# Rotary step on folded rows, squares summed on another engine, softmax rows in pairs: a hybrid encoder layer on one Trainium2 core

## The chip, the core and the metric

The kernel runs on one core of a Trainium2 chip. A core has TensorE (PE in the profile, with PEld for its weight loads), VectorE (DVE), ScalarE (ACT), GpSimd (POOL) and SyncE (SP), which here only issues transfers; ScalarE issues some transfers too. Each of these runs its instructions in the order in which they were built, and they wait for each other through semaphores. The metric is the device time of one execution in microseconds (us); less is better.

## The reference

One encoder layer in float32 on 1024 tokens of width 1024. One projection feeds two token mixers: group A is windowed attention (8 query heads, 2 key heads, a sink logit per head, rotary on the first 16 of 64 dimensions), group B is neighbourhood attention on a 16 x 64 grid of tokens. After that come an output projection, a gated MLP with a short convolution, and a last norm.

```python
def partial_rope(t, cos, sin):
    half = ROT_DIM // 2          # 8
    x1, x2 = t[..., :half], t[..., half:ROT_DIM]
    return concatenate([x1 * cos - x2 * sin, x2 * cos + x1 * sin, t[..., ROT_DIM:]], -1)

hn = rmsnorm(x, norm_mix)
proj = einsum('bsd,de->bse', hn, w_in)
qa, ka, va, qb, kb, vb = split(proj)
qa, ka = partial_rope(qa, cos, sin), partial_rope(ka, cos, sin)
# group A, per head: scores in a window of |i - j| <= 128, with the sink in the softmax
m = maximum(max(s, -1), sink)
p = exp(s - m)
o = einsum(p, v) / (sum(p, -1) + exp(sink - m))
# group B: p = softmax(scores + relative bias), o = einsum(p, v)
h = x + einsum(concat(rmsnorm(o_a), rmsnorm(o_b)), w_out)
h = h + conv_gated_mlp(rmsnorm(h, norm_ffn), ...)
out = rmsnorm(h, norm_final)
```

## The kernel before

Activations are kept transposed: 128 features on the partitions, 1024 tokens along the row, so a tile is 128x1024. To keep float32 precision each matmul operand is split into a rounded high part (ScalarE) and the rest (VectorE), and each product is three matmuls (`block`, lines 113 to 115).

**Head (up to 50 us).** The input's eight slices `xt` arrive; ScalarE makes the high part `xgh`, VectorE the low part `xgl` (`split_scaled`, line 126). The first two projection tiles use each slice as it comes; the third tile starts when all slices are there. Beside that ScalarE squares each slice and `squares(xts, nc.gpsimd)` sums the squares with seven additions on GpSimd (line 141). TensorE adds the sum over the partitions, and the resulting `rstd1` scales every projection as it leaves PSUM (`evacuate`, line 170).

**Projections.** `Project(m)` makes tile m. Of the first six, 0 and 3 hold one key head (partitions 0 to 63) and one value head, the others two query heads each. The columns are arranged so that in each head every eighth partition, from 0 and from 4, holds a rotated dimension: partition 8r holds x1 and 8r + 4 its partner x2. `post` finishes a tile: `split_v` transposes values, `rotate` does the rotary step, then `split_k` or `split_pair` make the parts and copies that the score matmuls need. `split_pair` leaves a query tile as two operand tiles, of which the first is complete only after its last copy, on SP (line 195); `split_k` issues `kb<-ka` (line 215) and `ka<-kb` (line 217) on SP as well.

**Rotation.** `rotate(t, n)` has two transfers on ScalarE's queue (line 182) put each row's partner into a zeroed tile `u`, then multiplies the whole tile by cosines (ones in the other rows, VectorE, line 183), `u` by signed sines (GpSimd, line 184), and adds them (VectorE, line 185). Two such tiles `u` take turns.

**Attention.** A unit is a block of queries. Score rows run in `softmax`: VectorE adds the mask and takes the minimum `nm` of the negated scores (line 284), ScalarE takes exponentials with their sum `sm` (line 288), VectorE the reciprocal (line 289), GpSimd scales the row (line 290); for group A GpSimd first copies the negated sink into the row's end (line 283). Two rows lie in one tile `p`. Later TensorE transposes the rows (`pt`), which are split again (`ph`, `pl`, lines 295 and 296) and multiplied with the values (`o`, lines 327 and 328). TensorE's order is written out by hand: projections are the filler between attention steps, by `FILL0`, `FILL1` and `RATES`. The order on the other engines and on the queues is made by a scheduler when the kernel is built, from priorities and from when it takes each input to be ready.

Tiles `rc`, `rs`, `u`, the third tile's weights, some tiles `p` and the attention outputs share eight buffers named `mix`.

Of the kernel before, what the change touches and what calls it, by code (L numbers as in the profile page):

```python
# [51 lines left out]
def hybrid_layer(tc, xT, w_in, w_out, w_gate, w_up, w_down, small, sink, rpb, consts, rope, out):  # L52
    nc = tc.nc
    with ExitStack() as ctx:
# [9 lines left out]
        spool = inner("stats", 6)  # L64
# [3 lines left out]
        def big(name, tag, dt=F32):  # L68
            return lpool.tile([128, S], dt, name=name, tag=tag, bufs=slots[tag])
# [65 lines left out]
        def squares(tiles, engine):  # L135
            acc = None
            for t in tiles:
                s2 = tmp("sq")
                nc.scalar.activation(s2, t, AF.Square)
                if acc is not None:  # L140
                    engine.tensor_tensor(s2, s2, acc, op=ALU.add)
                acc = s2
            return acc
# [29 lines left out]
                o = t[:, :].rearrange("p (b r c) -> p r b c", r=ROWS, c=8)[:, 8 * h:8 * h + 8]  # L173
                nc.vector.tensor_tensor(o, v(ps[:, :]), v(rstd1[:, tsl(h)]), op=ALU.mult)

        turned = []

        def rotate(t, n):
            u = turned[0]
            turned.append(turned.pop(0))  # L180
            for i in (0, 4):
                nc.scalar.dma_start(u[i:n:8], t[4 - i:n:8])
            nc.vector.tensor_tensor(t[0:n], t[0:n], rc[0:n], op=ALU.mult)
            nc.gpsimd.tensor_tensor(u[0:n], u[0:n], rs[0:n], op=ALU.mult)
            nc.vector.tensor_tensor(t[0:n], t[0:n], u[0:n], op=ALU.add)

        def split_pair(t):

# [46 lines left out]
        mix = [None] * 8  # L235
# [38 lines left out]
                return lpool.tile([128, 2, 386], F32, name="p", tag="mix", bufs=slots["mix"], padded_shape=[128, 2, 512])  # L274
            return apool.tile([128, 2, 386], F32, name="p", tag="p", bufs=5)

        def softmax(p, j, ps, n, bias, nsink=None):

            w = lambda ap: ap.rearrange("p (c w) -> p c w", w=128)
            with tc.high_priority(offset=50):  # L280
                nm, sm = spool.tile([128, 1], F32, name="nm"), spool.tile([128, 1], F32, name="sm")
                if nsink is not None:
                    nc.gpsimd.tensor_copy(p[:, j, n:n + 1], nsink)
                nc.vector.tensor_tensor_reduce(  # L284
                    out=w(p[:, j, 0:n]), in0=w(ps[:, 0:n]), in1=bias, scale=1.0, scalar=3e38 if nsink is None else nsink,
                    op0=ALU.add, op1=ALU.min, accum_out=nm)
                e = n if nsink is None else n + 1
                nc.scalar.activation(p[:, j, 0:e], p[:, j, 0:e], AF.Exp, bias=nm, scale=-1.0, accum_out=sm)  # L288
                nc.vector.reciprocal(sm, sm)  # L289
                nc.gpsimd.tensor_scalar(p[:, j, 0:n], p[:, j, 0:n], sm, 1.0, op0=ALU.mult, op1=ALU.mult)  # L290

        def split_pt(ps, n):
            ph = apool.tile([128, HALF], F32R, name="ph", tag="ph")
# [5 lines left out]
        def unit_window(g, b):  # L299

            cs, n = near(b), 128 * len(near(b))
            ps4 = [None] * 4
            mask = cst[:, K_MA:K_MA + 384].rearrange("p (c w) -> p c w", w=128)
            mask = mask[:, cs[0] - b + 1:cs[-1] - b + 2]
            st = {}

            def q_step(j):
                def go():
                    if j % 2 == 0:
                        st["p"] = pair_tile(True)  # L310
                    ps, _ = scores(qa[g, j // 2][j % 2], ka[g], b)
                    softmax(st["p"], j % 2, ps, n, mask, nsink[:, 4 * g + j:4 * g + j + 1])
                    ps4[j] = st["p"][:, j % 2, :]
                return go

            def t_step(i):
                def go():
                    if i == 0:
                        st["o"] = bank("o", "o")
                    pt = bank("pt", "pt")  # L320
                    for j in range(4):
                        nc.tensor.transpose(pt[:, j * 128:(j + 1) * 128], ps4[j][:, i * 128:(i + 1) * 128], ident)
                    ph, pl = split_pt(pt, HALF)

                    def v_step():
                        o, v = st["o"], va[g]
                        nc.tensor.matmul(o, v[:, cs[i], :], ph, start=i == 0, stop=False)
                        nc.tensor.matmul(o, v[:, cs[i], :], pl, start=False, stop=i == len(cs) - 1)
                        if i == len(cs) - 1:
                            leave()  # L330
                    return v_step
                return go

            def leave():
                ot = apool.tile([128, 2, 128], F32, name="ot", tag="ot", bufs=1, padded_shape=[128, 4, 128])
                o4 = st["o"][:, :].rearrange("p (j w) -> p j w", w=128)
                for e in range(2):
                    me, other = slice(64 * e, 64 * e + 64), slice(64 - 64 * e, 128 - 64 * e)
                    nc.scalar.activation(ot[me], o4[other, e::2, :], AF.Copy)
                    for i in range(2):  # L340
                        if mix[2 * g + i] is None:
                            mix[2 * g + i] = big("mixa", "mix")
                        nc.vector.tensor_tensor(mix[2 * g + i][me, b * 128:(b + 1) * 128], o4[me, e + 2 * i, :], ot[me, i, :], op=ALU.add)

            return [q_step(j) for j in range(4)], [t_step(i) for i in range(len(cs))]
# [19 lines left out]
        def units_grid(h):  # L365

            ps4 = [None] * NB
            st = {"begun": [False, False]}
            e = 64 * (h % 2)
            me, other = slice(e, e + 64), slice(64 - e, 128 - e)  # L370

            def q_step(b):
                def go():
                    if b == 0:
                        bias_of[h] = bias_of.pop(h, None) or bias_tiles(h)
                    if b == 4 and h < 7:
                        bias_of[h + 1] = bias_tiles(h + 1)
                    x = bias_of[h]
                    if b % 2 == 0:
                        st["p"] = pair_tile()  # L380
                    sel = slice(2, 5, 2) if b == 0 else slice(0, 3, 2) if b == NB - 1 else slice(1, 4)
                    ps, n = scores(qb[h], kb[h], b)
                    softmax(st["p"], b % 2, ps, n, x[:, sel, :])
                    ps4[b] = st["p"][:, b % 2, :]
                return go

# [111 lines left out]
        xts, sqs = [], []  # L498
# [41 lines left out]
        nc.sync.dma_start(par[:, C_SINK:C_END], sink.partition_broadcast(128))  # L540
        nsink = cpool.tile([128, 8], F32, name="nsink")
        nc.vector.tensor_scalar(nsink, par[:, C_SINK:C_END], -1.0, None, op0=ALU.mult)
        rc, rs = big("rc", "mix"), big("rs", "mix")
        nc.sync.dma_start(rc, rope[0])
        nc.sync.dma_start(rs, rope[1])

        for _ in range(2):
            u = big("u", "mix")
            nc.gpsimd.memset(u, 0.0)
            turned.append(u)  # L550

        banks = [[bank("pj", "pj") for _ in range(2)], [bank("o", "o") for _ in range(2)]]
        acc = None
        for k in range(KT):
            if k:
                xg[k] = split_scaled(xts[k], col(C_NMIX + k), "xg", "xg")
            for h in range(2):
                for p, ps in zip(first, banks):
                    block(ps[h], p.w[k], xg[k], h, k == 0, k == KT - 1)
        acc = squares(xts, nc.gpsimd)  # L560
        jobs = [Project(m) for m in range(2, 18)] + [OutA(d) for d in range(KT)]
        third = jobs[0]
        raw, hi, lo = big("raw3", "mix"), big("whi3", "mix", F32R), big("wlo3", "mix", F32R)
# [84 lines left out]
        for g in range(2):  # L648
            for b in range(NB):
                q, t = unit_window(g, b)  # L650
# [49 lines left out]
        for u in range(len(flat)):  # L700
            q, t, need, kind = flat[u]
# [412 lines left out]
        for i, f in enumerate(FO[HEAD:]):  # L1114
            u = Gated(f)
# [99 lines left out]
        for i, (p, j, c) in enumerate(order):  # L1215
            prepare(i + 6, i + 4)
            f, n = PARTS[c]
# [4 lines left out]
            ps = banks[p, j]  # L1222
# [48 lines left out]
def _constants():  # L1271
    import numpy as np

    f = np.float32
    consts = np.zeros((128, K_END), f)
    consts[:, K_ID:K_ID + 128] = np.eye(128, dtype=f)
    q, k = np.arange(128)[:, None], np.arange(128)[None, :]
    ma = np.zeros((128, 3, 128), bool)
    ma[:, 0], ma[:, 1], ma[:, 2] = k >= q, True, k <= q
    consts[:, K_MA:K_MA + 384] = np.where(ma, 0, MASKED).reshape(128, 384)  # L1280
    rq, cq, rk, ck = q // 8, q % 8, k // 8, k % 8
    r0 = np.clip(rq - KH // 2, 0, ROWS - KH)
# [7 lines left out]
    rope = np.zeros((2, 128, S), f)  # L1290
    rope[0] = 1.0
    for e in (0, 64):
        rope[0, e:e + 64:8], rope[0, e + 4:e + 64:8] = cos, cos
        rope[1, e:e + 64:8], rope[1, e + 4:e + 64:8] = -sin, sin
    return consts, rope


# [45 lines left out]
```

## Time and profile before

| What | Value |
|---|---|
| median of 3 runs | 1141.33 us (1141.04 to 1143.16) |
| profiled execution | 1136.96 us, span 1135.0 us |
| granted TensorE clock, mean | 0.986 |
| busy: TensorE, VectorE, ScalarE, GpSimd | 1088.1, 874.7, 550.2, 149.1 us |
| up to 130 us: seven additions of squares on GpSimd (line 141) | 19.6 us |
| up to 130 us: six products with sines on GpSimd (line 184) | 16.9 us |
| up to 130 us: VectorE's two operations of six rotations (lines 183, 185) | 9.7 and 9.7 us |

Rows of the timeline read: start in us, duration in us, engine, line, operation, output and inputs, shapes, count, and in brackets the engine's idle time just before and who ended it. SPq and ACTq are the transfers that SyncE and ScalarE issue. In rows of groups the number behind the bar is busy time in us, then the mean duration of one in ns, then idle time ahead of them. In rows of windows each engine's busy us stands with its count of instructions, and behind them the granted clock, the transfers' share and GB/s. In the list of transfers the last number is the median time in us from issue to landing.

### The profile page before, as it was taken

What the parts mean: (1) busy time and instruction counts of PE and PEld (TensorE: products, weight loads), DVE (VectorE), ACT (ScalarE), POOL (GpSimd) and SP (SyncE); (2) the same over time, 40 slices, a digit from 0 to 9 for tenths busy, and PEclk for the clock granted to TensorE, in tenths of its full rate; (3) what the DMA queues carried; (4) which work ended last, traced back from release to release, by engine and by line L of the source; (5) the groups of instructions that cost most, each with busy time, mean ns of one, the idle gap of its engine ahead of it and who ended that gap; (6) DMA issues with size and microseconds to landing.
All of it is one profiled execution on the core that took longest, in us unless ns stands there. A gap on an engine that the chain in (4) does not pass through costs nothing.

```text
span 1135.0 us, 15044 instructions
## 1 busy us (share of the span) xinstructions
PE 1088.1 (96%) x5124; PEld 903.0 (80%) x5124; DVE 874.7 (77%) x1594; ACT 550.2 (48%) x1033; POOL 149.1 (13%) x233
## 2 busy tenths in 40 slices
PE   7989999999999989999899999999999899999995
PEld 5867788888878878888688888888888688888884
DVE  6687888766689667899988778877887778886843
ACT  6235677655767534445443334333433554543531
POOL 4634533233223100000000000000000000000001
PEclk8999999999999999999999999999999999999998
DMA  7242120233305317402542223222322799775723
GB/s 273 72 119 74 48 57 28 73 95 89 78 28 150 101 47 241 146 31 96 192 131 103 107 89 129 94 103 93 123 101 93 232 319 298 260 226 163 261 78 148
DMA packets 65294, 147.17 MB, mean 130 GB/s; under 512 B 7969, under 2 KB 14113, under 8 KB 65217
## 3 DMA queue, kind: packets, MB, share of 16 engines
q1 hardware_dynamic: 56256, 121.17, 34.1%
q10 hardware_dynamic: 8960, 25.04, 5.8%
q8 instruction: 40, 0.66, 0.2%
q14 instruction: 38, 0.30, 0.1%
HBM read 104.37 MB, written 28.57 MB: 117 GB/s over the span
## 4 chain that ended last, share of the span: by engine, by line
PE 82%; DVE 8%; DMA 3%; issue 3%; ACT 2%; POOL 1%; SPq 0%; POOLq 0%; ACTq 0%; DVEq 0%
PE dn L785 6%; PE dn L786 6%; PE dn L787 6%; PE pj L113 6%; PE pj L114 6%; PE pj L115 6%; PE z L785 5%; PE z L787 5%; PE z L786 5%; PE x L785 3%; PE x L786 3%; PE x L787 3%; PE y L787 3%; PE y L785 3%; PE y L786 3%; PE s L266 3%
## 5 line engine op out<-in xcount | busy, mean ns | idle before, releaser
L774 ACT ACTIVATE whi<-ws 128x512 fp32r<-128x512 f32 (+1 forms) x100 | 60.1, 623 | 125.4 <-DVE ws L891 85.5
L785 PE MATMUL dn<-xd,whi 128*128 128x512 f32 x308 | 120.0, 390 | 0.0
L787 PE MATMUL dn<-xd,wlo 128*128 128x512 f32 x308 | 119.8, 389 | 0.0
L786 PE MATMUL dn<-xd,whi 128*128 128x512 f32 x308 | 119.8, 389 | 0.0
L785 PE MATMUL z<-hg,whi 128*128 128x512 f32 x264 | 103.4, 392 | 2.4 <-DVE gs L941 2.4
L787 PE MATMUL z<-hg,wlo 128*128 128x512 f32 x264 | 103.7, 393 | 0.2 <-DVE wlo L775 0.2
L113 PE MATMUL pj<-xgh,whi 128*128 128x512 f32 x248 | 103.8, 418 | 0.0
L786 PE MATMUL z<-hg,whi 128*128 128x512 f32 x264 | 103.3, 391 | 0.0
L290 POOL TENSOR_SCALAR p<-p,sm 128x384 f32<-128x384 f32 (+1 forms) x128 | 77.4, 606 | 192.1 <-DVE sm L289 165.3
L1197 POOL TENSOR_TENSOR y<-y,wide 128x512 f32<-128x512 f32 x4 | 5.1, 1280 | 734.1 <-ACT y L1196 734.1
L288 ACT ACTIVATE p<-p,nm 128x385 f32<-128x385 f32 (+3 forms) x128 | 74.9, 586 | 49.4 <-DVE nm L284 43.9
L114 PE MATMUL pj<-xgl,whi 128*128 128x512 f32 x248 | 97.8, 394 | 0.3 <-DVE xgl L126 0.3
L115 PE MATMUL pj<-xgh,wlo 128*128 128x512 f32 x248 | 98.1, 396 | 0.0
L775 DVE TENSOR_TENSOR wlo<-raw,whi 128x512 fp32r<-128x512 f32 (+1 forms) x102 | 66.5, 671 | 22.1 <-ACT whi L774 21.1
L774 ACT ACTIVATE whi<-raw 128x512 fp32r<-128x512 f32 (+1 forms) x102 | 61.0, 612 | 46.3 <-DMA raw<-in_w_down_dram 11.1
L775 DVE TENSOR_TENSOR wlo<-ws,whi 128x512 fp32r<-128x512 f32 (+1 forms) x100 | 66.9, 681 | 19.8 <-ACT whi L774 19.7
L296 DVE TENSOR_TENSOR pl<-pt,ph 128x384 fp32r<-128x384 f32 (+2 forms) x108 | 63.2, 588 | 21.5 <-ACT ph L295 20.2
L295 ACT ACTIVATE ph<-pt 128x384 fp32r<-128x384 f32 (+2 forms) x108 | 55.3, 514 | 40.6 <-PE pt L395 29.4
L1098 ACT ACTIVATE xd<-xd 128x512 fp32r<-128x512 f32 x77 | 46.9, 626 | 54.1 <-DMA xd<-x 50.7
L787 PE MATMUL y<-hg,wlo 128*128 128x512 f32 x176 | 69.4, 394 | 2.2 <-DVE wlo L775 2.2
L785 PE MATMUL y<-hg,whi 128*128 128x512 f32 x176 | 69.1, 393 | 1.9 <-ACT whi L774 1.9
L785 PE MATMUL x<-hg,whi 128*128 128x512 f32 x176 | 68.8, 391 | 1.4 <-ACT c L925 1.4
(201 smaller groups left out, 2721.9 us busy)
## 6 DMA issues: line engine op xcount, KB each, us to landing
xd<-x SPq DMA_DIRECT2D x77, 256.0 KB, 4.9
raw<-in_w_down_dram SPq DMA_DIRECT2D x72, 256.0 KB, 3.5
raw<-in_w_gate_dram SPq DMA_DIRECT2D x22, 512.0 KB, 3.4
raw<-in_w_up_dram SPq DMA_DIRECT2D x22, 512.0 KB, 5.6
x<-c ACTq DMA_DIRECT2D x22, 512.0 KB, 2.9
raw<-in_w_in_dram SPq DMA_DIRECT2D x32, 256.0 KB, 2.7
raw<-in_w_down_dram SPq DMA_DIRECT2D x36, 192.0 KB, 3.9
x<-t ACTq DMA_DIRECT2D x11, 512.0 KB
```

The costliest lines, as they stand in the source:

```text
L113: nc.tensor.matmul(ps, w[0], x[0][:, tsl(h)], start=first, stop=False)
L114: nc.tensor.matmul(ps, w[0], x[1][:, tsl(h)], start=False, stop=False)
L115: nc.tensor.matmul(ps, w[1], x[0][:, tsl(h)], start=False, stop=last)
L288: nc.scalar.activation(p[:, j, 0:e], p[:, j, 0:e], AF.Exp, bias=nm, scale=-1.0, accum_out=sm)
L290: nc.gpsimd.tensor_scalar(p[:, j, 0:n], p[:, j, 0:n], sm, 1.0, op0=ALU.mult, op1=ALU.mult)
L295: nc.scalar.activation(ph[:, 0:n], ps[:, 0:n], AF.Copy)
L296: nc.vector.tensor_tensor(pl[:, 0:n], ps[:, 0:n], f32(ph[:, 0:n]), op=ALU.subtract)
L774: nc.scalar.activation(hi, src, AF.Copy)
L775: nc.vector.tensor_tensor(lo, src, f32(hi[:, :, :]), op=ALU.subtract)
L785: nc.tensor.matmul(ps, w[0], x[0], start=first and i == 0, stop=False, skip_group_check=True)
L786: nc.tensor.matmul(ps, w[0], x[1], start=False, stop=False, skip_group_check=True)
L787: nc.tensor.matmul(ps, w[1], x[0], start=False, stop=last and i == len(ws) - 1, skip_group_check=True)
```

## The change

- Rotation: two transfers per tile on ScalarE's queue fold the 16 (or 8) rows of x1, and those of x2, over 128 (or 64) partitions, 128 tokens each, into a tile `f`. VectorE makes two products with sines (128 columns each), one with cosines and one sum (256 columns each), and two transfers on SP bring the rows back to their places. GpSimd has no part in it, and the rows that aren't rotated are not touched. The table of angles is folded in the same way, in one tile `turns` of 512 columns that is filled; the two zeroed tiles `u` and their fills go.
- `squares` of the input: the seven additions go from GpSimd to VectorE.
- `softmax`: for two rows of one tile `p` there is one copy of the two sinks, one reciprocal of two columns, and the two scalings follow the second row's exponential.

```diff
         def rotate(t, n):
-            u = turned[0]
-            turned.append(turned.pop(0))
-            for i in (0, 4):
-                nc.scalar.dma_start(u[i:n:8], t[4 - i:n:8])
-            nc.vector.tensor_tensor(t[0:n], t[0:n], rc[0:n], op=ALU.mult)
-            nc.gpsimd.tensor_tensor(u[0:n], u[0:n], rs[0:n], op=ALU.mult)
-            nc.vector.tensor_tensor(t[0:n], t[0:n], u[0:n], op=ALU.add)
+            m = slice(0, n)
+            f, u = folded[0]
+            folded.append(folded.pop(0))
+            rows = lambda s: t[4 * s:n:8].rearrange("a (c w) -> a c w", w=128)
+            fold = lambda s: f[m, s]
+            for s in range(2):
+                nc.scalar.dma_start(fold(s), rows(s))
+            for s in range(2):
+                nc.vector.tensor_tensor(u[m, s], f[m, 1 - s], rs[m, s], op=ALU.mult)
+            nc.vector.tensor_tensor(f[m], f[m], rc[m], op=ALU.mult)
+            nc.vector.tensor_tensor(f[m], f[m], u[m], op=ALU.add)
+            for s in range(2):
+                nc.sync.dma_start(rows(s), fold(s))
...
-        def softmax(p, j, ps, n, bias, nsink=None):
+        def softmax(st, j, ps, n, bias, nsink=None):
...
-                nm, sm = spool.tile([128, 1], F32, name="nm"), spool.tile([128, 1], F32, name="sm")
-                if nsink is not None:
-                    nc.gpsimd.tensor_copy(p[:, j, n:n + 1], nsink)
+                nm = spool.tile([128, 1], F32, name="nm")
+                if j == 0:
+                    st["sm"], st["n"] = spool.tile([128, 2], F32, name="sm"), [n, n]
+                sm, st["n"][j] = st["sm"], n
+                if nsink is not None and j == 0:
+                    nc.gpsimd.tensor_copy(p[:, 0:2, n:n + 1], nsink.rearrange("p (j o) -> p j o", o=1))
...
-                nc.scalar.activation(p[:, j, 0:e], p[:, j, 0:e], AF.Exp, bias=nm, scale=-1.0, accum_out=sm)
-                nc.vector.reciprocal(sm, sm)
-                nc.gpsimd.tensor_scalar(p[:, j, 0:n], p[:, j, 0:n], sm, 1.0, op0=ALU.mult, op1=ALU.mult)
+                nc.scalar.activation(p[:, j, 0:e], p[:, j, 0:e], AF.Exp, bias=nm, scale=-1.0, accum_out=sm[:, j:j + 1])
+                if j == 1:
+                    nc.vector.reciprocal(sm, sm)
+                    for i, m in enumerate(st["n"]):
+                        nc.gpsimd.tensor_scalar(p[:, i, 0:m], p[:, i, 0:m], sm[:, i:i + 1], 1.0, op0=ALU.mult, op1=ALU.mult)
...
-        rc, rs = big("rc", "mix"), big("rs", "mix")
-        nc.sync.dma_start(rc, rope[0])
-        nc.sync.dma_start(rs, rope[1])
+        quarters = lambda t: t[:, :].rearrange("p (a s w) -> p a s w", a=4, s=2)
+        turns = quarters(big("turns", "mix"))
+        rc, rs = turns[:, 0], turns[:, 1]
+        nc.sync.dma_start(turns[:, 0:2], rope)
         for _ in range(2):
-            u = big("u", "mix")
-            nc.gpsimd.memset(u, 0.0)
-            turned.append(u)
+            t = quarters(big("f", "mix"))
+            folded.append((t[:, 0], t[:, 1]))
...
-        acc = squares(xts, nc.gpsimd)
+        acc = squares(xts, nc.vector)
```

More of the change, by code (lines that the diff above doesn't have):

```diff
@@ L174, in evacuate @@
                 nc.vector.tensor_tensor(o, v(ps[:, :]), v(rstd1[:, tsl(h)]), op=ALU.mult)
-        turned = []
+        folded = []
         def rotate(t, n):
-            u = turned[0]
-            turned.append(turned.pop(0))
-            for i in (0, 4):
-                nc.scalar.dma_start(u[i:n:8], t[4 - i:n:8])
-            nc.vector.tensor_tensor(t[0:n], t[0:n], rc[0:n], op=ALU.mult)
-            nc.gpsimd.tensor_tensor(u[0:n], u[0:n], rs[0:n], op=ALU.mult)
-            nc.vector.tensor_tensor(t[0:n], t[0:n], u[0:n], op=ALU.add)
+            m = slice(0, n)
[11 more added lines that the diff above has]
+                nc.sync.dma_start(rows(s), fold(s))
         def split_pair(t):
@@ L275, in pair_tile @@
             return apool.tile([128, 2, 386], F32, name="p", tag="p", bufs=5)
-        def softmax(p, j, ps, n, bias, nsink=None):
+        def softmax(st, j, ps, n, bias, nsink=None):
             w = lambda ap: ap.rearrange("p (c w) -> p c w", w=128)
+            p = st["p"]
             with tc.high_priority(offset=50):
-                nm, sm = spool.tile([128, 1], F32, name="nm"), spool.tile([128, 1], F32, name="sm")
-                if nsink is not None:
-                    nc.gpsimd.tensor_copy(p[:, j, n:n + 1], nsink)
+                nm = spool.tile([128, 1], F32, name="nm")
[4 more added lines that the diff above has]
+                    nc.gpsimd.tensor_copy(p[:, 0:2, n:n + 1], nsink.rearrange("p (j o) -> p j o", o=1))
                 nc.vector.tensor_tensor_reduce(
-                    out=w(p[:, j, 0:n]), in0=w(ps[:, 0:n]), in1=bias, scale=1.0, scalar=3e38 if nsink is None else nsink,
+                    out=w(p[:, j, 0:n]), in0=w(ps[:, 0:n]), in1=bias, scale=1.0, scalar=3e38 if nsink is None else nsink[:, j:j + 1],
                     op0=ALU.add, op1=ALU.min, accum_out=nm)
                 e = n if nsink is None else n + 1
-                nc.scalar.activation(p[:, j, 0:e], p[:, j, 0:e], AF.Exp, bias=nm, scale=-1.0, accum_out=sm)
-                nc.vector.reciprocal(sm, sm)
-                nc.gpsimd.tensor_scalar(p[:, j, 0:n], p[:, j, 0:n], sm, 1.0, op0=ALU.mult, op1=ALU.mult)
+                nc.scalar.activation(p[:, j, 0:e], p[:, j, 0:e], AF.Exp, bias=nm, scale=-1.0, accum_out=sm[:, j:j + 1])
[3 more added lines that the diff above has]
+                        nc.gpsimd.tensor_scalar(p[:, i, 0:m], p[:, i, 0:m], sm[:, i:i + 1], 1.0, op0=ALU.mult, op1=ALU.mult)
         def split_pt(ps, n):
@@ L311, in go @@
                     ps, _ = scores(qa[g, j // 2][j % 2], ka[g], b)
-                    softmax(st["p"], j % 2, ps, n, mask, nsink[:, 4 * g + j:4 * g + j + 1])
+                    softmax(st, j % 2, ps, n, mask, nsink[:, 4 * g + j - j % 2:4 * g + j - j % 2 + 2])
                     ps4[j] = st["p"][:, j % 2, :]
@@ L382, in go @@
                     ps, n = scores(qb[h], kb[h], b)
-                    softmax(st["p"], b % 2, ps, n, x[:, sel, :])
+                    softmax(st, b % 2, ps, n, x[:, sel, :])
                     ps4[b] = st["p"][:, b % 2, :]
@@ L1289, in _constants @@
     cos, sin = np.cos(ang).astype(f), np.sin(ang).astype(f)
[L1290 to L1294, printed above, removed]
+    fold = lambda x: np.concatenate([x.reshape(64, 128)] * 2)
+    rope = np.zeros((128, 2, 2, 128), f)
+    rope[:, 0, 0], rope[:, 0, 1], rope[:, 1, 0], rope[:, 1, 1] = fold(cos), fold(cos), fold(-sin), fold(sin)
     return consts, rope
```

## The prediction

> **What bounds the kernel now.** I read the page first, for the engine that is busy and the chain that ended last.
>
> ```profile
> span 1135.0 us, 15044 instructions
> ...
> PE 1088.1 (96%) x5124; PEld 903.0 (80%) x5124; DVE 874.7 (77%) x1594; ACT 550.2 (48%) x1033; POOL 149.1 (13%) x233
> ...
> PE 82%; DVE 8%; DMA 3%; issue 3%; ACT 2%; POOL 1%; SPq 0%; POOLq 0%; ACTq 0%; DVEq 0%
> ...
> L290 POOL TENSOR_SCALAR p<-p,sm 128x384 f32<-128x384 f32 (+1 forms) x128 | 77.4, 606 | 192.1 <-DVE sm L289 165.3
> ```
>
> TensorE is busy for 96% and the change leaves its instructions and their order as they are. So it can only move the 47 us in which TensorE waits, or its clock. The table of windows says where those waits are; all code that is touched runs before 460 us.
>
> ```profile
> 5.00:23.00 18.00, 13.14 (x39) 8.95 (x40) 13.51 (x11) 12.82 (x16) 10.14 (x4) 0.81 0.95 354
> ...
> 75.00:90.00 15.00, 11.99 (x49) 9.83 (x50) 9.02 (x24) 5.60 (x15) 4.09 (x7) 0.89 0.39 98
> 90.00:130.00 40.00, 35.80 (x186) 29.16 (x185) 35.31 (x95) 26.34 (x64) 21.94 (x42) 1.00 0.23 58
> 130.00:200.00 70.00, 68.76 (x374) 58.79 (x374) 59.35 (x186) 50.19 (x125) 23.36 (x65) 1.00 0.15 42
> 200.00:460.00 260.00, 251.72 (x1339) 212.50 (x1338) 188.36 (x451) 149.17 (x329) 54.59 (x82) 0.99 0.37 106
> ```
>
> First number after the stretch is its length, then busy PE, PEld, DVE, ACT, POOL, then the granted clock. TensorE idles 3.0 us in 75 to 90, 4.2 in 90 to 130 (DVE busy 88%), 1.2 in 130 to 200, 8.3 in 200 to 460. These and the head are the places to work through.
>
> **Squares on VectorE (head).** TensorE's timeline:
>
> ```profile
> 20.51 0.39 PE L113 MATMUL pj<-xgh,w 128*128 128x512 f32 x1
> 22.44 0.50 PE L114 MATMUL pj<-xgl,w 128*128 128x512 f32 x1 [1.54 <-DVE xgl L126]
> ...
> 25.77 0.50 PE L114 MATMUL pj<-xgl,whi 128*128 128x512 f32 x1 [0.32 <-DVE xgl L126]
> ...
> 27.57 0.51 PE L115 MATMUL o<-xgh,wlo 128*128 128x512 f32 x1 [0.58 <-DVE wlo L109]
> ...
> 37.46 0.39 PE L113 MATMUL s<-xgh,whi 128*128 128x512 f32 x1
> ...
> 42.67 0.39 PE L115 MATMUL s<-xgh,wlo 128*128 128x512 f32 x1
> ```
>
> Between 20.51 and 37.46 lie five slices of x, twelve matmuls each. The 24 matmuls from 37.46 to 42.67 start 0.227 us apart, so 60 of them need 13.6 us, and 17.0 were taken: 3.3 us were lost to late VectorE results, directly (2.44 in the three brackets) or at the restarts. VectorE and GpSimd there:
>
> ```profile
> 11.64 1.28 DVE L126 SCALAR_TENSOR_TENSOR xgl<-xt,par,xgh 128x1024 fp32r<-128x1024 f32 x1 [1.84 <-ACT xgh L125]
> 13.62 2.63 DVE L126 SCALAR_TENSOR_TENSOR xgl<-xt,par,xgh 128x1024 fp32r<-128x1024 f32 x1 [0.70 <-ACT xgh L125]
> ...
> 18.97 7.94 DVE L126 SCALAR_TENSOR_TENSOR xgl<-xt,par,xgh 128x1024 fp32r<-128x1024 f32 x3
> ...
> 119.08 1.23 DVE L185 TENSOR_TENSOR t<-t,u 128x1024 f32<-128x1024 f32 x1 [1.17 <-POOL u L184]
> ```
> ```profile
> 12.63 12.01 POOL L141 TENSOR_TENSOR sq<-sq 128x1024 f32<-128x1024 f32 x4 [11.66 <-ACT sq L139]
> ```
>
> The split of one slice costs 1.28 us until GpSimd's adds begin, and 2.6 beside them. Without GpSimd I take 1.25, and 1.23 for each add that moves to VectorE (the row of an add of that size). In the built order VectorE then has split 1, add, split 2, a weight split, add, split 3: from 11.64 with these prices split 3 ends at about 18.2 (before: 22.4), ahead of its first use at 20.7. The later ones follow at about 1.9 us a slice against 2.7 on TensorE, and the last of the seven adds ends near 33, ahead of the row sums at 42.9 - 3.3 = 39.6. So **-3.3 us**, ends -2.4 (the brackets alone) and -3.4. The halved rope load and the dropped memsets lie behind this and are taken at nothing; what hides them is that the third tile's weights are not waited for in either order.
>
> **Rotation (49 to 78 us).** Four small VectorE operations take the place of two of 1024 elements and GpSimd's product, and two transfers on SP are added. What waited here:
>
> ```profile
> 74.04 0.28 PE L266 MATMUL s<-kb,q 128*128 128x256 f32 x1
> 77.66 0.36 PE L266 MATMUL s<-ka,q 128*128 128x256 f32 x1 [3.33 <-DMA q<-t]
> ```
> ```profile
> 73.69 2.57 DVE L183 TENSOR_TENSOR t<-t,rc 64x1024 f32<-64x1024 f32 x1
> 76.19 0.47 DVE L284 CUSTOM_DVE_ANT_0 p<-s,cst,nsink 128x256 f32<-128x256 f32 x1
> ```
> ```profile
> 59.89 1.06 ACT L214 ACTIVATE ka<-t 64x1024 fp32r<-64x1024 f32 x1 [7.53 <-DVE t L185]
> ...
> 71.16 0.64 ACT L230 ACTIVATE v<-vt 128x256 fp32r<-128x256 f32 x2
> 71.82 1.28 ACT L288 ACT_TABLE_LOAD   x1
> 76.70 0.51 ACT L288 ACTIVATE p<-p,nm 128x257 f32<-128x257 f32 x1 [3.60 <-DVE nm L284]
> ```
> ```profile
> 60.98 0.52 SPq L215 DMA_DIRECT2D kb<-ka  x1
> ...
> 74.70 0.46 SPq L195 DMA_DIRECT2D q<-t  x1
> ```
>
> Attention's first two score rows run at 73.69; the third needs the second query tile, whose last copy is issued at 74.70 and used at 77.66, 2.96 later. One would expect the shorter rotation to bring this forward. The built order says otherwise. That copy now stands on SP behind the key copy of the fourth tile (the kb copy that L215 issues), which waits for ScalarE's ka; and ka now stands on ScalarE behind the first two exponentials, whose table load has moved behind the wait for the first score minimum. So the third score row comes to hang on the first: scores done 74.1, minimum +0.47 = 74.6, table +1.28 = 75.9, two exponentials at 0.51 = 76.9, v copies +0.64 = 77.5, ka +1.06 = 78.6, kb issue +0.52 = 79.1, q copy 2.96 = 82.1. That is **+4.4 us** against 77.66. VectorE's part is freer (the L183 of 2.57 is gone ahead of the minimum, as counted).
>
> For the new transfers and operations:
>
> ```profile
> q<-t SPq DMA_DIRECT2D x8, 256.0 KB, 4.1
> ...
> u<-t ACTq DMA_DIRECT2D x8, 64.0 KB, 1.9
> ```
> ```profile
> L343 DVE TENSOR_TENSOR mixa<-o,ot 64x128 f32<-64x128 f32 x14 | 3.5, 278 | 0.3 <-ACT ot L339 0.2
> ```
>
> A fold or unfold moves the 64 KB of u<-t in pieces of 512 bytes, which no row shows: between 1.9 us (same bytes) and 4.1 (four times the bytes); I take 1.9, nearest in size; below that nothing speaks for a gain. A small operation costs about 0.28, twice that for 256 columns. At 1.9 the first queries are ready near 68 and the fourth tile's unfold lands near 73, both ahead of their use (73.7 and 77.5), so both are hidden; at 4.1 the unfold lands near 77.8 and costs 0.3. If the q copy itself takes 4.1 instead of 2.96, the gap grows by 1.1: ends +3.2 and +5.5, the lower one for earlier minimum and overlapped copies.
>
> **Clock.** In 75 to 90 the granted clock is 0.89, which is half clock for 15 x 0.11 / 0.5 = 3.3 us after a 3.3 us gap; in 5 to 23 it is 0.81, half clock for 6.8 us. A stretch of s us at half clock costs TensorE s/2. After an idle of 8 us I expect 3.3 to 5.5 us at half clock, partly under score rows that wait anyway: **+0.4 us**, ends 0 and +1.6 (6.8 instead of 3.3, halved). The Trainium skill (TensorE: Matmul & The Clock Gate, Why this matters for your kernels) warns against TensorE gaps over about 3 us, after which the array runs at half clock until a window of about 3.4 us has been busy; by it alone the longer gap adds at most that one window, an estimate of 1.7 us. The trace agrees in that its two cold stretches are one and two times 3.3 to 3.4 us long.
>
> **Rotations inside attention (90 to 130).**
>
> ```profile
> 121.47 0.50 PE L328 MATMUL o<-pl,v 128*128 128x512 f32 x1 [1.41 <-DVE pl L296]
> 123.18 0.33 PE L322 MATMUL pt<-cst,p 128*128 128x128 f32 x1 [0.18 <-POOL p L290]
> ```
> ```profile
> 92.17 2.28 DVE L183 TENSOR_TENSOR t<-t,rc 128x1024 f32<-128x1024 f32 x1
> ...
> 95.56 1.48 DVE L185 TENSOR_TENSOR t<-t,u 128x1024 f32<-128x1024 f32 x1
> ```
> ```profile
> 115.58 3.46 POOL L184 TENSOR_TENSOR u<-u,rs 128x1024 f32<-128x1024 f32 x1
> ```
>
> The fifth tile's rotation takes 3.76 us of VectorE and the sixth holds GpSimd for 3.46, with probability tiles queued behind. Both go; the fifth's small operations fall ahead of attention's second batch, the sixth's cost 0.28 x 4 + 0.56. DVE's load in this stretch falls by some 5 of 35 us, under the share of 130 to 200, where TensorE idles 1.24 of 70. At that rate 0.7 of the 4.2 us stays: **-3.5 us**, ends -1.8 (the copies of the split stay in the same places) and -4.2. **Pairs and the rest (130 to 460):** 64 of 128 reciprocals and 32 of 64 sink copies go, all off the path; DVE's waits shrink a little: **-1.0 us**, ends -3.0 and +0.5 (a row waits for its pair).
>
> **Sum:** -3.3 + 4.4 + 0.4 - 3.5 - 1.0 = -3.0 us. The profiled execution took 1136.96 us (span 1135.0), the median of the runs is 1141.33; I carry the difference over: 1133.96 for such an execution, **1138.3 us** for the median. Its own range, with ends added where they don't all fall together, is 1134.5 to 1142.
>
> **Rivals.**
> *Pairs turn into a wait (slower).* In each pair GpSimd scales the first row only after the second exponential, so the second row is ready one scaling, 0.61 us (L290), later. If TensorE's transposes met that at ten pairs, it costs 6 us: +3.0, 1144.3; from nine pairs on it decides. For it: every pair is touched. Against it: only one 0.18 us wait on GpSimd stands in the trace, and a unit of other work lies between scores and transposes.
> *The split is slow for another reason (slower).* If 2.6 us comes from the transfers that fill memory at the time (DMA share 0.95 in 5 to 23), VectorE gets 8.6 us of adds and no relief: -3.0 + 3.3 + about 5 = +5.3, 1146.6. It decides if the split's mean stays over 1.9 us. Against it: the split at 11.64 took 1.28 under the same transfers. The Trainium skill (SBUF — State Buffer, SBUF: two separate sides) says that transfers and engines have separate ports; by that this case is void.
> *The gap stays as it is (faster).* If the second query copy isn't held back, for instance because ka's wait is short, the gap and the clock terms go: -7.8, 1133.5. For it: the rotation's data is ready 3 us sooner. Against it: each of the queues runs in its written order.
>
> **How the numbers follow.** About 0.2% (2.3 us) is what a measurement of this kernel can tell. The forecast has 0.70, of which 0.40 below -2.3, 0.25 within, 0.05 above; pairs 0.12 and slow split 0.06, both slower; the gap stays 0.12, faster. Faster 0.52, same 0.25, slower 0.23. Leaving out the last two rivals (0.18), the range goes from 1134.5 to the pairs' 1144.4.
>
> **What would show it.** Right: no bracket on xgl from 20 to 28 and splits of 1.25 us; the row sums near 39.6; a TensorE gap of about 8 us starting near 70.8 and ended by a q copy, with a table load right behind the first score minimum; no GpSimd operation over 1 us between 50 and 130; TensorE idle under 1.5 us in the 40 us after the gap's restart. Wrong: a gap of under 5 us or none (the order isn't what holds the copy), splits over 1.9 us, or TensorE's transposes waiting for p at many pairs.

## The result, and the profile after

The changed kernel takes 1137.3 us (median of 6 runs, 1135.27 to 1137.96); the kernel before, in runs beside it, 1141.3 (1140.22 to 1143.16). The ratio is 0.9964, 95% interval 0.9949 to 0.9979: a gain of 2.4 to 5.8 us. The prediction said 1138.3. The profiled execution took 1135.27 us (span 1133.5) where the one before took 1136.96.

First the page of the changed kernel: busy times, the chain that ended last, and the scaling of rows on GpSimd.

```profile
span 1133.5 us, 14918 instructions
...
PE 1087.3 (96%) x5124; PEld 904.3 (80%) x5124; DVE 853.2 (75%) x1549; ACT 549.9 (49%) x1033; POOL 105.9 (9%) x186
...
PE 87%; DVE 6%; DMA 2%; ACT 2%; issue 1%; SPq 0%; POOLq 0%; ACTq 0%; DVEq 0%
...
L303 POOL TENSOR_SCALAR p<-p,sm 128x384 f32<-128x384 f32 (+1 forms) x128 | 73.2, 584 | 237.1 <-DVE sm L301 217.9
```

VectorE has lost 21.5 us and GpSimd 43, and TensorE's idle time went from 46.9 to 46.2 us. So the question is the same as before: where does TensorE wait? The table of windows of the changed kernel:

```profile
5.00:23.00 18.00, 14.14 (x43) 10.18 (x44) 12.87 (x15) 12.65 (x16) 0.00 (x0) 0.81 0.94 345
75.00:90.00 15.00, 9.93 (x37) 8.33 (x38) 5.81 (x15) 4.30 (x11) 2.46 (x5) 0.69 0.40 99
90.00:130.00 40.00, 39.24 (x205) 32.35 (x204) 32.91 (x94) 26.79 (x65) 12.45 (x29) 1.00 0.30 79
```

GpSimd has nothing to do in 5 to 23 (10.14 us before). TensorE idles 0.8 us in 90 to 130 (before: 4.2), but more around 75, where the granted clock is 0.69 (0.89). The rows of TensorE's timeline there:

```profile
71.11 0.28 PE L273 MATMUL s<-kb,q 128*128 128x256 f32 x1
79.91 0.55 PE L273 MATMUL s<-ka,q 128*128 128x256 f32 x1 [8.52 <-DMA q<-t]
```

The wait on the query copy grew from 3.33 to 8.52 us. Its chain of waits, each piece with start and length:

```profile
71.19 0.30 DVE p L295
...
71.77 1.28 ACT L299
...
73.47 0.68 ACT p L299 x3
74.15 0.54 ACT v L237 x2
74.69 0.95 ACT ka L221
...
75.66 0.46 SPq L222
...
76.21 3.56 DMA q<-t
```

That is link by link the chain that the prediction wrote down: first minimum, table load (L299 at 71.77), exponentials, v, ka, the issue of the key copy (L222), the query copy, third score row.

TensorE's instructions stand in the same order in both kernels, so each can be compared with itself. Start in the kernel before, how much later (+) or earlier (-) it starts in the changed one, and what the forecast's terms add up to there:

| start before, us | where | measured | forecast |
|---|---|---|---|
| 20.3 | first two slices of x done | +1.06 | 0 |
| 30.7 | slices of x done | -2.29 | -3.3 |
| 74.0 | second score row | -2.93 | -3.3 |
| 77.7 | third score row | +2.25 | +1.1 |
| 86.0 | half clock is over | +2.27 | +1.5 |
| 134.5 | sixth tile's rotation is past | -1.39 | -2.0 |
| 400.9 | end of attention | -1.71 | -3.0 |
| 1135.0 | end of the span | -1.5 | -3.0 |

### The profile page after: what moved, and what is told of

It is laid out like the page before. It is cut to its first block, busy times and chain, and to the rows that moved or that the text cites. A ratio compares the mean times of both kernels' runs of the same rounds, so it can differ in the third digit from the quotient of the medians.

```text
span 1133.5 us, 14918 instructions
## 1 busy us (share of the span) xinstructions
PE 1087.3 (96%) x5124; PEld 904.3 (80%) x5124; DVE 853.2 (75%) x1549; ACT 549.9 (49%) x1033; POOL 105.9 (9%) x186
## 4 chain that ended last, share of the span: by engine, by line
PE 87%; DVE 6%; DMA 2%; ACT 2%; issue 1%; SPq 0%; POOLq 0%; ACTq 0%; DVEq 0%
PE pj L113 7%; PE pj L114 7%; PE pj L115 7%; PE dn L797 6%; PE dn L799 6%; PE dn L798 6%; PE z L797 4%; PE z L798 4%; PE z L799 4%; PE s L273 3%; PE x L797 3%; PE x L798 3%; PE x L799 3%; PE y L799 3%; PE y L798 3%; PE y L797 3%
## 5 line engine op out<-in xcount | busy, mean ns | idle before, releaser
L299 ACT ACTIVATE p<-p,nm 128x385 f32<-128x385 f32 (+3 forms) x128 | 75.1, 587 | 55.5 <-DVE nm L295 51.5
L303 POOL TENSOR_SCALAR p<-p,sm 128x384 f32<-128x384 f32 (+1 forms) x128 | 73.2, 584 | 237.1 <-DVE sm L301 217.9
```

The lines of the kernel that those rows point to most:

```text
L303: nc.gpsimd.tensor_scalar(p[:, i, 0:m], p[:, i, 0:m], sm[:, i:i + 1], 1.0, op0=ALU.mult, op1=ALU.mult)
```

## Experiments: one part alone

Each kernel is the one before with one part of the change. The edits are the hunks of the diff above.

**Squares on VectorE alone.**

```diff
-        acc = squares(xts, nc.gpsimd)
+        acc = squares(xts, nc.vector)
```

> The kernel before with the seven adds of squares on VectorE and nothing else of the change. Theory (the split of x was slow because GpSimd worked beside it): splits of 1.28 us throughout the head, no wait on xgl between 20 and 28 us, TensorE 2.3 to 2.4 us earlier from 38 us on, as in the changed kernel; the wait on the query copy stays near 3.3 us, and the lead is still 2.4 at 150 us: about 1138.9 us, 0.998 of before. Rival (the transfers into memory make the split slow): splits stay near 2.6, the adds come on top, 3 to 5 us slower. Second rival (the lead is swallowed by the wait on the query copy): the wait grows to 5.7 us and the time is that of before.

1137.64 us, ratio 0.9976 (0.9961 to 0.9992). The splits of x and the adds between 10 and 33 us, as groups on VectorE, here:

```profile
L126 DVE SCALAR_TENSOR_TENSOR xgl<-xt,par,xgh 128x1024 fp32r<-128x1024 f32 x7 | 8.9, 1279 | 2.8 <-ACT xgh L125 2.8
L141 DVE TENSOR_TENSOR sq<-sq 128x1024 f32<-128x1024 f32 x7 | 8.6, 1228 | 0.2
```

and in the kernel before, with the adds on GpSimd:

```profile
L126 DVE SCALAR_TENSOR_TENSOR xgl<-xt,par,xgh 128x1024 fp32r<-128x1024 f32 x7 | 16.5, 2385 | 2.5 <-ACT xgh L125 2.5
...
L542 DVE TENSOR_SCALAR nsink<-par 128x8 f32<-128x8 f32 x1 | 2.4, 2368 | 0.0
```

Seven splits and seven adds take 17.5 us of VectorE; the splits alone took 16.5 beside GpSimd. The transfers are the same in both, so the rival that blamed them falls. No wait on xgl is left between 20 and 28 us, and TensorE is 2.39 us ahead at 38 us. But the second rival has part of the truth: the wait on the query copy grew.

```profile
76.27 0.55 PE L266 MATMUL s<-ka,q 128*128 128x256 f32 x1 [4.38 <-DMA q<-t]
```

With the half clock around it, the lead falls from 2.44 us at 74 us to 0.91 at 98. The chain of waits says what held: the pair's first copy (`q<-q`, issued at 68.85) took 4.45 us to land, and the last copy, which overwrites what the first one reads, was issued after that, at 73.31. In the kernel before these issues are 3.42 us apart. Why the landing took longer here isn't shown: the transfers around it are issued at the same distances in both kernels, and with the pairs alone too, where the two issues are 4.01 us apart. So the longer wait may be scatter of this one execution and not the squares' doing.

**Rotation alone.**

> The kernel before with the folded rotation alone (GpSimd still adds the squares, softmax rows one by one). Theory (the new rotation alone makes the order of the queues in which the last query copy stands behind the key copy, and it alone frees VectorE and GpSimd at 100 to 134 us): nothing up to 49 us, a wait of 8 to 8.7 us on the query copy that ends near 82.2 us, so 4.8 to 5.3 us behind the kernel before there, then 3.5 to 3.9 won back between 98 and 134 us: 1 to 1.5 us slower at 150 us, about 1142.5 us. Rival (the pairs make that order, or the relief): the wait stays near 3.3 us, and at 150 us it is 3.7 us faster if the relief is the rotation's and 0 if it is the pairs'.

1140.74 us, ratio 1.0006 (0.9992 to 1.0019).

```profile
83.77 0.55 PE L273 MATMUL s<-ka,q 128*128 128x256 f32 x1 [8.51 <-DMA q<-t]
```

The wait is that of the changed kernel, and TensorE falls 5.0 us further behind across it (+0.94 at 74 us to +5.97 at 98; the wait ends later than expected, since TensorE came to it late, see the last section). Between 98 and 134 us it wins back 2.8, less than the 3.5 to 3.9 expected. So both the loss and the relief belong to the rotation, but in this trace 2.2 us of the loss stay. The times show none of it, 1140.74 us where 1142.5 was expected; the interval, from 0.9 us faster to 2.2 slower, leaves room for it.

**Pairs alone, and everything but the pairs.**

> The kernel before with the softmax rows in pairs alone. Theory (off the path, the relief at 98 to 134 us is the rotation's): the wait on the query copy stays near 3.3 us, TensorE within 0.5 us of before at 150 us, time within 0.1%. Rival (pairs delay the second row by one scaling of 0.6 us): waits of TensorE on p in the transposes of the window layers, 1 us or more in all, slower. Second rival (pairs brought the relief): 3 to 4 us faster at 150 us.

> The changed kernel with the softmax rows one by one again (a reciprocal, a sink copy and a scaling for each row); squares and rotation stay changed. Theory (the pairs are off the path on both sides): TensorE within 0.5 us of the changed kernel from 100 to 380 us, wait on the query copy 8.5 us as there, time within 0.15% of the changed kernel. Rival (the pairs are worth something only where VectorE is otherwise relieved): waits on pl and nm at 98 to 134 us grow by 1 us or more in all, 1 to 3 us slower than the changed kernel.

Pairs alone: 1141.76 us, ratio 1.0008 (0.9996 to 1.002). The wait on the query copy is 3.73 us, TensorE loses 0.7 us between 74 and 134 us, a little more than expected, and none of its waits of 0.15 us or more up to 460 us is on p. All but the pairs: 1136.88, ratio 0.9966 (0.9954 to 0.9977), where the full change has 0.9964; from 57 to 150 us TensorE moves by 0.15 us against the changed kernel. In the times the pairs are worth nothing that these runs can tell, either way. But the 0.15 us is a balance: without the pairs TensorE gains 0.5 us on the changed kernel where the half clock ends at 82.1 us instead of 84.4, and loses 0.8 from 100 to 130 us, where it waits 0.90 us for pl instead of 0.30 and 0.75 for score minima instead of 0.31.

## Experiments: the wait on the query copy

These start from the changed kernel.

**The key copy off SP.**

```diff
-            nc.sync.dma_start(f32(b[o:o + 64, :]), f32(a[e:e + 64, :]))
+            nc.scalar.dma_start(f32(b[o:o + 64, :]), f32(a[e:e + 64, :]))
```

> The changed kernel with one transfer moved: the first key copy (kb from ka) is issued by ScalarE, right behind the operation that makes ka, so that nothing on SP stands between the last two query copies but a weight load that is free to go. Theory (the last query copy is late because it stands behind the key copy on SP): the copy is issued near 74.3 us instead of 76.2 and lands near 77.9; the wait of TensorE falls from 8.5 to 6.5 us and the time by about 2 us against the changed kernel, to about 1135.3. Rival (the copy is late for its own data or its own landing): the wait stays at 8 to 8.5 us. Second rival (ScalarE, now with an issue of 0.5 us in its row, delays the exponentials): the wait shortens but the third row's exponential or the transposes at 92 us come later by as much.

1134.4 us, ratio to before 0.9948 (0.9929 to 0.9968). But the wait is nearly what it was, and this is a miss. TensorE's row, then the chain of waits ahead of it:

```profile
77.75 0.55 PE L273 MATMUL s<-ka,q 128*128 128x256 f32 x1 [8.33 <-DMA q<-t]
```
```profile
70.12 1.15 DVE t L199
...
71.28 0.50 SPq L201
...
71.84 0.57 SPq L105
...
72.46 5.15 DMA q<-t
```

All of this kernel runs 2.0 us early after a faster head; against that, the copy was issued 1.75 us earlier than in the changed kernel, and then took 5.15 us instead of 3.56. Right ahead of it now stands a weight load of 256 KB (L105), and the chain comes to it from the low part (L199), which stands behind the first minima on VectorE: the key copy wasn't the only link that held. The interval overlaps the changed kernel's, and in the traces this edit accounts for 0.55 us between 57 and 150 us; the 2.0 are the head's, which the edit doesn't touch.

**The weight load behind it as well.** The load is queued on SP behind the last query copy; the key copy stays on ScalarE.

> As the run with the key copy moved to ScalarE, and the weight load that stood between the last two query copies on SP is issued behind the last one. Theory (there the copy was issued 1.75 us earlier and yet landed late because 256 KB of weights went into the transfer engines 0.6 us ahead of it): issued right behind its neighbour, 0.5 us after it, it lands in 3.0 to 3.7 us instead of 5.15; the wait of TensorE falls from 8.3 to 5.9 to 6.6 us, and it is 2 us faster than the changed kernel up to 150 us at an equal head. Rival (landing is slow because the three query copies themselves fill the engines): landing stays at 4.5 us or more, wait 7.3 us or more.

1134.91 us, ratio 0.9945 (0.9926 to 0.9963). The chain and TensorE's row:

```profile
72.23 3.79 DMA q<-t
```
```profile
76.16 0.55 PE L278 MATMUL s<-ka,q 128*128 128x256 f32 x1 [6.39 <-DMA q<-t]
```

Landing took 3.79 us, a touch over what was expected, the wait is 6.39 us, and from 57 to 150 us TensorE gains 2.06 us on the changed kernel. So both hold the copy: its place on SP, and 256 KB that go into the transfer engines just ahead of it. The Trainium skill (DMA: Bandwidth & Descriptors, Issuing engines are not separate DMA queues) says that transfers run on the same 16 engines whichever engine issues them. The run with the key copy moved agrees: there ScalarE issues the key copy at 73.69, while the query copy is on its way, and the transfers' share is 1.01, 1.01 and 1.06, which is full, in the three us from 74 us on. Another issuer freed SP and not the way of the bytes.

**The order mended.** Three instructions of the pair come first: its low part ahead of the first minima, of the fourth tile's rotation and of the fifth tile's evacuation on VectorE; its copies ahead of the fourth tile's transfers on SP. `issue_after(x)` sets what is built within it behind x on x's engine, in order alone, without a wait. The edit in short, without the conditions that pick the tiles:

```diff
+        # low, end: the pair's low part (VectorE) and its last copy (SP)
-                    rotate(t, 64)
-                    ka[g] = split_k(t, 0)
+                    with issue_after(low), issue_after(end):      # fourth tile
+                        rotate(t, 64)
+                        ka[g] = split_k(t, 0)
...
-                    softmax(st, j % 2, ps, n, mask, ...)
+                    with issue_after(low):                        # first two rows
+                        softmax(st, j % 2, ps, n, mask, ...)
```

The fifth tile's evacuation is set behind `low` and its second weight load behind `end` in the same way.

> The changed kernel with the order alone mended: the second query tile's low part stands ahead of the first score minima, of the fourth tile's rotation and of the fifth tile's evacuation on VectorE; on SP its three copies stand ahead of the fourth tile's unfolds and key copies. No instruction is added. Theory (the order of the queues is what makes the wait, the low part's place on VectorE above all): low part at 68 us instead of 72.0, last query copy issued near 71 instead of 76.2, landed 3 to 3.6 us later at 74 to 74.5; the wait of TensorE falls from 8.5 to 2.6 to 3.2 us, and the time by 5 to 7 us, to 1130 to 1132. Rival (the landing is what counts: three copies of 256 KB and a weight load share the transfer engines, as in the run with the key copy moved, where landing took 5.15 us): the copy lands at 76, wait 4.5 us, time 3.5 to 4 us down. Second rival (the wait moves to the fourth tile's keys or the fifth tile's projection): waits of 2 us or more between 75 and 130 us that the changed kernel doesn't have.

1130.82 us, ratio 0.9913 (0.9888 to 0.9938). VectorE, SP and TensorE:

```profile
66.97 1.23 DVE L209 SCALAR_TENSOR_TENSOR t<-t,q 128x1024 fp32r<-128x1024 f32 x1 [3.32 <-ACT q L207]
```
```profile
69.78 0.46 SPq L212 DMA_DIRECT2D q<-t  x1
```
```profile
72.76 0.35 PE L288 MATMUL s<-ka,q 128*128 128x256 f32 x1 [2.27 <-ACT p L314]
```

Against the changed kernel the low part starts 5.0 us earlier (there 72.01), the copy is issued 6.4 us earlier (76.21), and the wait is 2.27 us. The profile names an exponential as what ended it, but the third row has no exponential among its inputs; the copy issued 2.98 us before is the likelier one. The gain on the changed kernel, 6.3 us from 57 to 150 us, stays whole at 340 us. No new wait stands behind it.

**Four projection blocks ahead of the third row**, alone and with the order.

```diff
-        run_q(q_until(1, 4 + AHEAD))
-        fill(FILL1)
+        run_q(q_until(1, 2))
+        fill(4)
+        run_q(q_until(1, 2 + AHEAD))
+        fill(FILL1 - 4)
```

> The changed kernel with only the four blocks moved, the order not mended by hand (the last query copy comes to stand behind a weight load and ahead of the key copy). Theory (the copy lands 77.5 to 79.9 whatever TensorE does): TensorE works 2.7 us longer before it waits, the wait falls from 8.5 to 3.4 to 5.8 us, time 2.7 to 5 us below the changed kernel. Rival (given back later, as above): 1 us or less gained.

> As the run before, and four projection blocks (of the twelve that follow the sixth score row) set between the second and the third score row, 2.7 us of TensorE's work. Theory: they cover what is left of the wait, which falls to 0 to 0.6 us; TensorE never idles for 3 us there, so the half clock of 74 to 84 us goes too: 2.5 to 4.5 us below the run with the order alone, 1127 to 1129. Rival (given back later: the first transposes wait for the later rows' probabilities, or the projection waits for its weights): new waits near 80 to 92 us of 1.5 us or more, and at most 1 us gained.

Blocks alone: 1135.04 us, ratio 0.9951 (0.9933 to 0.997); the wait is 5.46 us and the gain 2.55 us from 57 to 150 us, just under the lower end. Order and blocks: **1127.39 us, ratio 0.9885 (0.9867 to 0.9903)**, the fastest version here and below both kernels, though its interval overlaps that of the order alone. The third row doesn't wait any more. The rival has a part, though: the fifth row waits for the third's minimum. TensorE, VectorE and ScalarE of that run:

```profile
76.91 0.60 PE L288 MATMUL s<-ka,q 128*128 128x384 f32 x1 [2.55 <-DVE nm L310]
```
```profile
72.68 0.69 DVE L114 TENSOR_TENSOR wlo<-raw,whi 128x512 fp32r<-128x512 f32 x1 [1.62 <-ACT whi L113]
73.29 0.48 DVE L310 CUSTOM_DVE_ANT_0 p<-s,cst,nsink 128x256 f32<-128x256 f32 x1
...
76.37 0.47 DVE L310 CUSTOM_DVE_ANT_0 p<-s,cst,nsink 128x256 f32<-128x256 f32 x1
```
```profile
72.02 0.63 ACT L113 ACTIVATE whi<-raw 128x512 fp32r<-128x512 f32 x1 [5.20 <-issue]
72.67 1.28 ACT L314 ACT_TABLE_LOAD   x1
```

The second row's minimum (73.29) stands on VectorE behind a weight split that waits for ScalarE, and the third's follows at 76.37. From 57 to 150 us 7.7 us are gained on the changed kernel, against 6.3 with the order alone: 1.4 us more in the traces, where 2.5 to 4.5 were expected and the medians differ by 3.4. The half clock, which was expected to go, stays for 3.4 us, from 77.0 to 80.4.

**The minima ahead of the weight split.** As the last one, with higher priority for the first rows' softmax.

```diff
-            with tc.high_priority(offset=50):
+            with tc.high_priority(offset=500 if len(pair_ends) == 2 else 50):
```

> As the run with the order mended and four blocks set ahead of the third row, with the softmax operations of the first rows given precedence over the weight split (the second row's minimum stands ahead of it on VectorE instead of behind). Theory (in that run the fifth row waited 2.55 us for the third row's minimum, which stood on VectorE behind a minimum that stood behind a weight split that waited for ScalarE): minimum of the second row at 71 us instead of 73.3, third row's by 0.4 us or more earlier, wait 2.2 us or less, time 0.3 to 1 us below 1127.4. Rival (the fourth tile's rotation and the table load of 1.28 us hold VectorE's queue all the same): wait stays at 2.5 us, no difference.

1129.13 us, ratio 0.9894 (0.9868 to 0.992). The rival is right:

```profile
76.27 0.69 PE L288 MATMUL s<-ka,q 128*128 128x384 f32 x1 [2.65 <-DVE nm L310]
```

The second minimum moved to 70.6 us, but the third still stands at 75.74, behind the fourth tile's rotation and the reciprocal, which waits for exponentials that stand behind ScalarE's weight conversion and the table load. To clear that, ScalarE's order would have to change; it wasn't tried.

## Why the prediction was right

**Head.** The splits were forecast at 1.25 us and the adds at 1.23; they took 1.28 and 1.22. Between 20.3 and 30.7 us TensorE gained 3.35 us (+1.06 to -2.29), forecast -3.3. What was missing is ahead of that: the second slice's high part came 0.36 us later (bracket 2.66 instead of 2.21), and the half clock lasted to 19.5 us instead of 17.7. TensorE was 1.06 us late there, so the row sums stood at 40.6 and not at 39.6. That lateness isn't the change's. In the eight other traces with the adds on VectorE TensorE comes to this row between 1.18 us earlier and 0.95 us later than in the kernel before, so it is scatter between executions; the stretch from this row to the end of the slices takes 7.03 us in all nine of them, against 10.37 in the kernel before. The exclusive hold between VectorE and GpSimd that the Trainium skill states (SBUF — State Buffer, SBUF: two separate sides) fits the 2.37 us that an operation of eight columns took beside GpSimd; alone it took 0.17. It ran from 31.98 to 34.35 us, and GpSimd's addition beside it ended at 34.32.

**Rotation and wait.** Right in mechanism and nearly in size: forecast +4.4, measured +5.18 (-2.93 to +2.25), within the ends. The query copy was priced at 2.96 us and took 3.70 from issue to use, which is most of the difference. The runs qualify the cause. The order of SP is one of two holds, as the copy off SP showed; the other is what goes into the transfer engines ahead of the copy. And mending the order took the low part's place on VectorE as well as SP's, a link that the prediction's chain doesn't have; VectorE's place alone wasn't tried.

**Folds and unfolds.** Taken at 1.9 us, they land later, but within the ends. The list of transfers of the changed kernel, 40 to 140 us:

```profile
f<-t ACTq DMA_DIRECT2D x8, 64.0 KB, 2.3
t<-f SPq DMA_DIRECT2D x8, 64.0 KB, 2.8
```

TensorE waits for none of them directly.

**Clock.** Forecast +0.4; between the third row and 86 us nothing was lost (+2.25 to +2.27). The half clock lasted from 74.2 to 84.4 us, but 5.7 us of that lay in the wait itself; 4.5 us of work in it stand against 3.4 before, and part of that is score rows that wait for one another anyway.

**Rotations inside attention.** Forecast -3.5, measured -3.66 (+2.27 to -1.39). GpSimd's two products of 2.9 us and the waits on pl (3.6 us before) are gone:

```profile
104.46 0.50 PE L341 MATMUL o<-pl,v 128*128 128x512 f32 x1 [0.30 <-DVE pl L309]
```

Some 0.8 us of this came with the pairs: over the same stretch the run without them gains 2.9 us and the run with the rotation alone 2.8, so the rotation's own part was forecast too high. VectorE's load fell by 2.4 us there, not by the 5 that the prediction reckoned with, so the share was a poor yardstick for the relief. That it hung on when the rotation's work stood in the queue fits this, but no run here tests it.

**Pairs and the rest.** Forecast -1.0, measured -0.3 up to the end of attention. This term was mis-sized for its stretch: what the pairs bring, some 0.8 us, lies ahead of it, in the term above.

**The total.** On the profiled executions the sum was -1.7 us instead of -3.0. Too hopeful were the wait (0.8) and the rest (0.7), and the head's start added 1.06, the scatter named above; too cautious were the clock (0.4), the relief inside attention (0.2) and 30 to 74 us, where 0.64 us weren't forecast at all: VectorE evacuates the fourth tile without delay, and a wait of 0.4 us on that is gone. That the median still came within 1.0 us is partly luck: the difference of 4.37 us between profile and median of the kernel before was carried over, and is 2.0 us for the changed kernel. Two errors offset each other, and runs of one kernel scatter by some 3 us here and by up to 9.6 in the runs above (1125.29 to 1134.88 with the order mended). Of the rivals none occurred: the wait didn't stay, the splits took 1.28 us, and no row's pair held TensorE for more than 0.15 us.

The parts taken alone give about -2.7, +0.7 and +0.9 us by their ratios, so -1.1 against -4.0 together; the intervals are too wide to be sure of the difference. One reason would fit the traces: alone, much of the squares' lead was lost at the query copy, which hung on a landing; in the changed kernel the wait hangs on the first score row, which moves with TensorE, and the lead is kept. As that landing may be scatter, this isn't shown.

## What to carry to other kernels

A shorter operation can lengthen a wait, because the scheduler that sets the queues' order works from its own idea of when things are ready: read the built order around each wait before pricing an edit, and write down the chain link by link. When a transfer is late, look at what stands ahead of it on its issuer, at what its data waits for, and at how many bytes go into the transfer engines just before it; taking away one hold shows the next. Work that TensorE can do anyway, set into a wait, is worth what it covers only if the rows behind it don't come to stand behind its weights.

## What the runs showed that was not expected

In some executions the clock halves where no wait of TensorE is longer than 0.8 us. Windows of the run with the rotation alone, right behind the row sums, which are the same code in all these kernels:

```profile
46.00:48.00 2.00, 1.22 (x8) 1.14 (x8) 1.64 (x4) 0.52 (x2) 1.93 (x6) 0.72 0.09 34
48.00:50.00 2.00, 2.00 (x9) 1.81 (x9) 0.38 (x2) 0.60 (x1) 0.00 (x0) 0.50 0.39 102
50.00:52.00 2.00, 2.00 (x10) 1.62 (x9) 1.22 (x2) 0.00 (x0) 0.00 (x0) 0.93 0.07 24
```

and of the kernel before, where TensorE comes to the row sums 0.04 us earlier, at full clock:

```profile
46.00:48.00 2.00, 1.22 (x11) 1.14 (x11) 1.68 (x4) 0.48 (x2) 1.63 (x2) 1.00 0.04 15
48.00:50.00 2.00, 2.00 (x12) 1.66 (x12) 1.29 (x3) 0.60 (x1) 0.00 (x0) 1.00 0.23 55
50.00:52.00 2.00, 2.00 (x14) 1.76 (x13) 0.29 (x2) 0.41 (x2) 0.00 (x0) 1.00 0.32 87
```

The waits of TensorE are the same in both, 0.61 and 0.78 us, yet 1.5 us are lost in the first. Of the eleven traced executions of kernels other than the one before, four lose 1.5 to 1.6 us there, this one among them. The Trainium skill (TensorE: Matmul & The Clock Gate, What's actually happening) says that the window in which activity is judged is about 3.4 us long and runs freely. That would explain why the same instructions fall on either side; no run here moves the window, so it isn't shown. Together with the scatter at the head it makes a difference of 2 us between two single profiles unfit as evidence, which is why stages were compared from a common point above.
